# A two-block transformer on one core: fused convolution taps, a fixed engine for each weight half, and a planner that knows of the interface VectorE and GpSimd share

## The chip, the cores and the metric

The kernel runs on one core of one Trainium2 chip. A core has five engines that run side by side, each with its own queue of instructions: TensorE (PE in the profile, its weight loads PEld), VectorE (DVE), ScalarE (ACT), GpSimd (POOL) and SyncE (SP), which here only issues DMA transfers. The metric is device time of one execution in microseconds (us), lower is better; several runs are made and the median is taken.

## The reference

Two transformer blocks are computed in float32 on 512 tokens of width 1024. The parts that matter here:

```python
# block 1, the mixer's gated convolution: 256 channels, 31 taps along the tokens
y = a * sigmoid(g)
y = causal_dwconv(y, conv_w, conv_b)          # y[t] = b + sum_k w[k] * y[t - 30 + k]
y = silu(standardize(y by heads of 64) * gn_g + gn_b)
# beside it in the mixer: spatial gating (4 heads) and an mLSTM (4 heads), then
h = x + concat(y_a, y_b, y_c) @ w_out
# then cross attention, conv_glu (w_up, w_down); block 2: sparse attention with pooling,
# MLP, gated linear attention, MLP:
h = relu(h @ mlp_w1) ** 2 @ mlp_w2
...
```

The work is almost all products of 512-token activations with weight matrices. Every weight is read from memory once.

## The kernel before

**Products in three parts.** TensorE multiplies float32r operands, so each float32 matrix is held as two float32r parts, hi and lo, whose sum is exact (class `Split`), and a product is three matmuls: hi·hi, hi·lo and lo·hi (`mm`). For activations `split` makes hi with ScalarE (a copy that rounds) and lo with VectorE (source minus hi). In the trace these parts end in h and l: `xth`, `xtl` are activations, `wh`, `wl` weights, `hid` a hidden layer's pair.

**Weights.** `wunit` streams one unit of weights (128 x 1024) into a raw buffer `wr` (three of them) by DMA, and splits it by halves of 512 columns into two pages `wh` and `wl`. The kernel has 625 such halves. For them `split(..., weights=True)` leaves the engine open: `wh` may be a ScalarE copy or a VectorE cast, `wl = wr - wh` may be VectorE or GpSimd, with 1.0 us (`BIAS`) held against VectorE:

```python
nc.add([[("scalar", "activation", (hi, src, AF.Copy), {})], [("vector", "tensor_copy", (hi, src), {})]],
       BIAS)
self.either("tensor_sub", lo, src, hi.bitcast(F32), bias=BIAS)
```

Pages come free when the last matmul that reads them is done, and a stage may have only 5 to 9 units at a time (`rules`), so conversions are bound to TensorE's progress.

**Taps.** `taps` is the 31-tap convolution for two groups of 128 channels (`gcv`, from `yp`). For each tap but the first, a product `tm = yp * w` is made on VectorE or ScalarE (whichever the plan picks), and GpSimd adds it: `gcv += tm`. That is 60 products and 60 sums, sprinkled among the other steps of the mixer.

**What sets the order.** No engine order is written by hand. All calls go to a `Recorder`; `Plan` then lays the recorded steps out in time with a price for each instruction (`price1`) and a time until others see its result (`price`), tile space, DMA and activation tables. `Plan.run` takes at each point the engine that can start soonest, and on it the ready step of the highest rank; where a step has several forms (`either`, or `nc.add` with two lists), it takes the engine that by its prices is done first. `improve` repeats this eight times with the latest starts as ranks and keeps the shortest plan. `emit` then issues all instructions in the plan's order (one line, so nearly the whole trace bears line L487), and where the plan leaves TensorE idle for more than 1 us it adds products that nothing reads (`warm`, in the trace `ps<-ident`, 128x512) to fill the time. The program so fixed is static: on the chip each engine goes through its own list in order and waits on semaphores.

**Stages.** mix (the mixer, with keys and values of the memory, `mem`, as filler), xattn, ffn, nsa, mlp0, gla, mlp1. Each ends in a projection and a norm by token tiles (`tail`).

Of the kernel before, what the change touches and what calls it, by code (L numbers as in the profile page):

```python
# [28 lines left out]
# room: pages of weights or of a split block, half pages, weights on their way in  # L29
# [5 lines left out]
BIAS = 1.0  # L35


class Op:
    """One step of the plan: instructions that one engine issues back to back."""
# [20 lines left out]
def run(ap):  # L60
    """Elements next to each other in a transfer."""
    n = 1
    for s, k in sorted((int(s), int(k)) for s, k in list(ap.ap)[1:]):
        if s != n:
            break
        n *= k
    return n


def region(ap):  # L70
    """The tile, the partitions and the set of elements (as bits) that an access touches."""
# [26 lines left out]
class Recorder:  # L98
    """Stands in for the engines: keeps what they are told to do for the plan."""
# [9 lines left out]
    def add(self, forms, bias=0.0):  # L109
        """forms: ways to do one step, each a list of calls to one engine; bias: time against VectorE's."""  # L110
# [17 lines left out]
        o.forms = [(f[0][0], f) + price(f) + (bias if f[0][0] == "vector" else 0.0,) for f in forms]  # L128
# [3 lines left out]
    @contextmanager  # L132
    def together(self):
        """Calls to one engine as one step."""
        self.held = []
        yield
        calls, self.held = self.held, None
        self.add([calls])
# [11 lines left out]
def price1(eng, m, args, kw):  # L150
# [5 lines left out]
    if eng == "tensor":  # L156
        if m == "transpose":
            return 0.109
        if "float32r" in str(args[1].dtype):
            return max(n, 2 * width(args[1])) / 2400.0 + 0.0025  # L160
# [26 lines left out]

def price(calls):
    """Time on the engine, and the time after it until others see the result."""
# [5 lines left out]
class Plan:  # L195
    """Orders the recorded steps: each engine takes the ready step with the longest way to the end."""
# [16 lines left out]
    def depend(self):  # L213
# [29 lines left out]
        # weights wait for an earlier unit's end, and nothing starts too far ahead of its use  # L243
# [17 lines left out]
        # late banks are taken when all that goes into them is there  # L261
# [30 lines left out]
    def rank(self):  # L292
        for o in reversed(self.ops):
            eng, _, d, lat, _ = o.forms[0]
# [12 lines left out]
    def run(self, prio=None):  # L307
        ops, N = self.ops, len(self.ops)
        P = prio or [o.prio for o in ops]
        free = dict.fromkeys(Recorder.ENGINES, 0.0)  # L310
        dma_issue = dma_data = 0.0
# [17 lines left out]
        def room(o):  # L329
            """Time from which the step's new tiles find room; None if they may not be taken yet."""  # L330
# [32 lines left out]
        for _ in range(N):  # L363
            best = None
            for e, q in queue.items():
# [4 lines left out]
                for i in q:  # L370
                    o = ops[i]
                    s = ready[i] if ready[i] > f else f
                    if mn is not None and s > mn:
                        continue
                    form = next(x for x in o.forms if x[0] == e)
                    if len(o.forms) > 1:
                        mine = s + form[2] + form[4]
                        if any(max(ready[i], free[x[0]]) + x[2] + x[4] < mine - 1e-9 for x in o.forms if x[0] != e):
# [30 lines left out]
            _, calls, d, lat, _ = form  # L409
# [7 lines left out]
            else:  # L417
# [4 lines left out]
                end = free[e] = s + d  # L422
            o.start, o.end, o.pick, o.room = s, end, calls, taken
# [19 lines left out]
    def improve(self, n):  # L443
        """Plans again with the last plan's latest starts as ranks, and keeps the best plan."""
# [8 lines left out]
    def late(self):  # L453
        """Latest starts of the steps when each engine keeps its order, as priorities."""
# [16 lines left out]
    def emit(self, tc, warm):  # L471
        """warm: calls that keep the array's clock up, for a bank about to be used."""
# [17 lines left out]
class Split:  # L490
    """A float32 matrix as two float32r parts whose sum is exact."""
# [11 lines left out]
class Duo:  # L503
    """Two 128-row blocks of a split matrix, as one operand of the vector engines and as blocks."""
# [6 lines left out]
class Block:  # L511
# [19 lines left out]
    # ---- room  # L531
    def rules(self, quota, banks=(2, 10), pages=(2, 1000), halves=(0, 1000)):
        """For the steps from here on: units of weights at a time; of each kind of room, what a step ahead of
        its turn leaves free for those before it, and how many of them it may pass."""
# [3 lines left out]
    def ps(self, late=False):  # L538
        """A bank; late: not taken before all that goes into it is there."""
# [1336 lines left out]
```

## Time and profile before

| | |
|---|---|
| median of 3 runs | 2028.74 us (2028.26 to 2033.82) |
| profiled execution: span from first to last instruction | 2026.6 us |
| mean granted TensorE clock | 0.982 |
| busy: PE / DVE / ACT / POOL | 1931.1 / 1283.8 / 804.4 / 714.8 us |
| instructions on DVE / ACT / POOL | 2366 / 1614 / 571 |
| DMA | 177.40 MB, mean 88 GB/s |

"Busy" is the time in which at least one instruction of the engine runs. Matmuls are pipelined: one of 512 columns is shown some 0.39 us long while the next starts 0.23 us after it, so a hole between matmuls is longer in truth than the idle time shown. The profile page names groups as `out<-in`, by tile names without buffer numbers.

### The profile page before, as it was taken

The page shows a single profiled execution, that of the slowest core. Times are in us where ns is not written, and L with a number is a line of the kernel's source. Part 1 is how long each engine was busy: PE and PEld are TensorE (multiplying, and loading weights), DVE is VectorE, ACT ScalarE, POOL GpSimd, SP SyncE. Part 2 cuts the span into 40 slices and gives each one's busy share as a digit, 9 for nine tenths or more (in the row PEclk, how much of TensorE's full clock was granted, in tenths as well). Part 3 has the DMA queues.
Part 4 walks back from the last instruction along what each step waited for, and adds up shares of the span by engine and source line. Part 5 has one row for each costly group of instructions (what it writes and reads, how often), then busy time and mean ns, then how long its engine had stood idle before and what let it go on. Part 6 is the DMA issues. An engine that isn't in the chain of part 4 may idle for free. (4 is left out here: it accounts for less than half of the span.)

```text
span 2026.6 us, 27236 instructions
## 1 busy us (share of the span) xinstructions
PE 1931.1 (95%) x10206; PEld 1632.6 (81%) x10206; DVE 1283.8 (63%) x2366; ACT 804.4 (40%) x1614; POOL 714.8 (35%) x571
## 2 busy tenths in 40 slices
PE   8978899999999999989999999999999999999998
PEld 7756778888888888878888777777999888778776
DVE  5899966564444456588984345467686774355457
ACT  4556435334322233576734223232465334122231
POOL 3767534213212333233644222233223234122232
PEclk9988999999999999999999999999999999999999
DMA  5212333223213333330332233332223322223231
GB/s 165 79 47 72 125 94 115 83 63 105 74 54 102 115 101 89 70 74 11 97 112 84 63 94 104 85 126 77 83 62 104 94 73 87 61 77 107 91 127 55
DMA packets 215470, 177.40 MB, mean 88 GB/s; under 512 B 25174, under 2 KB 194202, under 8 KB 215338
## 3 DMA queue, kind: packets, MB, share of 16 engines
q1 hardware_dynamic: 215338, 175.66, 29.6%
q8 instruction: 80, 1.31, 0.3%
q14 instruction: 52, 0.43, 0.1%
HBM read 173.54 MB, written 2.10 MB: 87 GB/s over the span
## 5 line engine op out<-in xcount | busy, mean ns | idle before, releaser
L487 POOL TENSOR_TENSOR wl<-wr,wh 128x512 fp32r<-128x512 f32 (+1 forms) x387 | 551.7, 1438 | 1093.3 <-PE ps L487 450.3
L487 PE MATMUL ps<-xth,wl 128*128 128x512 f32 (+1 forms) x1464 | 516.9, 353 | 4.9 <-DVE wl L487 4.3
L487 PE MATMUL ps<-xtl,wh 128*128 128x512 f32 (+1 forms) x1464 | 517.3, 353 | 3.8 <-DVE xtl L487 3.7
L487 PE MATMUL ps<-xth,wh 128*128 128x512 f32 (+1 forms) x1464 | 519.4, 355 | 0.1
L487 ACT ACTIVATE wh<-wr 128x512 fp32r<-128x512 f32 (+1 forms) x544 | 311.9, 622 | 462.9 <-PE ps L487 277.3
L487 PE MATMUL ps<-wh,hid 128*128 128x512 f32 (+1 forms) x1392 | 437.5, 392 | 1.4 <-ACT wh L487 1.3
L487 DVE TENSOR_TENSOR wl<-wr,wh 128x512 fp32r<-128x512 f32 x238 | 285.0, 1211 | 135.4 <-ACT wh L487 78.9
L487 PEld LDWEIGHTS ps<-xth,wl 128*128 128x128 f32 x1464 | 278.3, 190 | 47.0 <-DVE wl L487 5.8
L487 PEld LDWEIGHTS ps<-xtl,wh 128*128 128x128 f32 x1464 | 278.6, 190 | 44.6 <-DVE xtl L487 6.0
L487 PEld LDWEIGHTS ps<-xth,wh 128*128 128x128 f32 x1464 | 279.0, 191 | 40.1 <-ACT xth L487 0.5
L487 PEld LDWEIGHTS ps<-wh,hid 128*128 128x128 f32 x1392 | 261.1, 188 | 60.9 <-ACT wh L487 2.7
L487 PE MATMUL ps<-wl,hid 128*128 128x512 f32 (+1 forms) x696 | 275.0, 395 | 7.7 <-DVE wl L487 6.2
L487 DVE TENSOR_TENSOR x<-x,ps 128x512 f32<-128x512 f32 (+1 forms) x210 | 140.6, 677 | 155.7 <-PE ps L487 154.8
L487 PEld LDWEIGHTS ps<-wl,hid 128*128 128x128 f32 x696 | 131.2, 188 | 46.5 <-DVE wl L487 13.6
L487 DVE TENSOR_TENSOR r<-r 128x512 f32<-128x512 f32 x64 | 69.0, 1079 | 65.2 <-ACT r L487 64.7
L487 DVE CAST wh<-wr 128x512 fp32r<-128x512 f32 x81 | 45.8, 581 | 90.5 <-PE ps L487 83.7
L487 PE MATMUL ps<-wl,xth 128*128 128x256 f32 (+2 forms) x320 | 94.6, 296 | 1.3 <-DVE wl L487 1.0
L487 PE MATMUL ps<-wh,xth 128*128 128x256 f32 (+2 forms) x320 | 95.7, 299 | 0.0
L487 PE MATMUL ps<-wh,xtl 128*128 128x256 f32 (+2 forms) x320 | 94.3, 295 | 0.0
L487 POOL TENSOR_TENSOR gcv<-gcv,tm 128x511 f32<-128x511 f32 (+29 forms) x60 | 81.4, 1376 | 16.8 <-DVE tm L487 12.3
L487 DVE TENSOR_TENSOR hid<-r,hid 128x512 fp32r<-128x512 f32 x64 | 51.8, 810 | 43.0 <-ACT hid L487 42.4
L487 ACT ACTIVATE r<-ps 128x512 f32<-128x512 f32 x64 | 37.7, 589 | 90.6 <-PE ps L487 90.6
(355 smaller groups left out, 2718.2 us busy)
## 6 DMA issues: line engine op xcount, KB each, us to landing
wr<-in_mlp_w_dram SPq DMA_DIRECT2D x128, 512.0 KB
wr<-in_w_up_dram SPq DMA_DIRECT2D x44, 512.0 KB
wr<-in_c_w_in_dram SPq DMA_DIRECT2D x24, 512.0 KB
wr<-in_w_down_dram SPq DMA_DIRECT2D x22, 512.0 KB
wr<-in_w_in_dram SPq DMA_DIRECT2D x16, 512.0 KB
wr<-in_w_xkv_dram SPq DMA_DIRECT2D x16, 512.0 KB
wr<-in_w_out_dram SPq DMA_DIRECT2D x8, 512.0 KB
wr<-in_w_xq_dram SPq DMA_DIRECT2D x8, 512.0 KB
```

The source lines that it names most:

```text
L487: getattr(getattr(self.rec.nc, eng), method)(*args, **kw)
```

## The change

Docstrings and comments are dropped too, which moves line numbers (L487 becomes L509) and nothing else. The rest:

```diff
-BIAS = 1.0
+BIAS = 0.0
...
-        o.forms = [(f[0][0], f) + price(f) + (bias if f[0][0] == "vector" else 0.0,) for f in forms]
+        o.forms = [(f[0][0], f) + price(f) + (bias if f[0][0] == "vector" else 0.0, port(f)) for f in forms]
...
         if "float32r" in str(args[1].dtype):
-            return max(n, 2 * width(args[1])) / 2400.0 + 0.0025
+            return max(n / 2285.0 + 0.007, width(args[1]) / 1200.0 + 0.0025)
...
+def port(calls):
+
+    for eng, m, args, kw in calls:
+        if eng not in ("vector", "gpsimd") or m in ("memset", "iota", "dma_start"):
+            continue
+        out = kw["out"] if "out" in kw else args[0]
+        ins = [x for x in list(args[1:]) + [x for k, x in kw.items() if k not in ("out", "accum_out")] if is_ap(x)]
+        room = [x for x in ins if "PSUM" not in str(x.space) and width(x) > 1]
+        if eng == "gpsimd" or len(room) > 1:
+            return True
+        if m in ("tensor_copy", "tensor_scalar") and room and "PSUM" not in str(out.space):
+            return True
+    return False
...
@@ Plan.run
+        shared = 0.0
...
+                    form = next(x for x in o.forms if x[0] == e)
+                    if form[5] and shared > s:
+                        s = shared
                     if mn is not None and s > mn:
                         continue
-                    form = next(x for x in o.forms if x[0] == e)
                     if len(o.forms) > 1:
                         mine = s + form[2] + form[4]
-                        if any(max(ready[i], free[x[0]]) + x[2] + x[4] < mine - 1e-9 for x in o.forms if x[0] != e):
+                        if any(max(ready[i], free[x[0]], shared if x[5] else 0.0) + x[2] + x[4] < mine - 1e-9
+                               for x in o.forms if x[0] != e):
                             continue
...
                 end = free[e] = s + d
+                if locks:
+                    shared = end
...
@@ Block.split, weights=True
-                nc.add([[("scalar", "activation", (hi, src, AF.Copy), {})], [("vector", "tensor_copy", (hi, src), {})]],
-                       BIAS)
-                self.either("tensor_sub", lo, src, hi.bitcast(F32), bias=BIAS)
+                nc.scalar.activation(hi, src, AF.Copy)
+                nc.vector.tensor_sub(lo, src, hi.bitcast(F32))
...
@@ taps
-                        tm = self.s2("tm")
-                        nc.add([[("vector", "tensor_scalar", (tm[:, :n], yp[j][:, :n], w, None), dict(op0=OP.mult))],
-                                [("scalar", "activation", (tm[:, :n], yp[j][:, :n], AF.Copy), dict(scale=w))]])
-                        nc.gpsimd.tensor_add(gcv[j][:, t:], gcv[j][:, t:], tm[:, :n])
+                        nc.vector.scalar_tensor_tensor(gcv[j][:, t:], yp[j][:, :n], w, gcv[j][:, t:], op0=OP.mult,
+                                                       op1=OP.add)
```

So three things change. A tap is one VectorE instruction, `gcv = yp * w + gcv`. Of every weight half `wh` is ScalarE's and `wl` VectorE's. And the planner has one more resource, `shared`: a GpSimd step, a VectorE step with two SBUF inputs, and a VectorE copy or scalar step from SBUF to SBUF hold it, and none of them starts while another holds it. A 512-column matmul is also priced a little dearer. Since all of the order comes from the plan, every engine's order changes.

By count over the whole program: `wl` on POOL 387 before, 0 now; on DVE 238, now 625. `wh` on ACT 544, now 625; on DVE 81, now 0. Taps: 40 products on DVE, 20 on ACT and 60 sums on POOL before; 60 fused instructions on DVE now. POOL has 576 instructions before and 128 now, DVE 2368 and 2692, ACT 1484 and 1543. The filler products on PE (`ps<-ident 128x512`) are 38 before and 180 now; of these 24 and 173 stand in the mix stage.

**First place: DVE and PE ahead of the first q product of the mixer.** `xconv` is the convolved input of an mLSTM head, made by DVE (its lo part) and taken by PE with `wh_165`, `wl_166` (the weights of q, k and v); `ps_168` is q's bank. DVE's rows up to `xconv`, before:

```order
L487 TENSOR_SCALAR tm_200<-yp_145,cols_78 128x509
L487 TENSOR_SCALAR tm_253<-yp_154,cols_78 128x504
L487 TENSOR_TENSOR wl_306<-wr_304,wh_305 128x384
L487 TENSOR_SCALAR tm_219<-yp_145,cols_78 128x508
L487 TENSOR_SCALAR tm_255<-yp_154,cols_78 128x503
L487 SCALAR_TENSOR_TENSOR gs_132<-gs_132,gs_133 4x512
L487 TENSOR_TENSOR xc_206<-ps_204,xc_206 128x512
L487 TENSOR_TENSOR xconv_140<-cv_138,xconv_140 128x512
```

and now:

```order
L509 SCALAR_TENSOR_TENSOR gcv_173<-yp_154,cols_78,gcv_173 128x491
L509 SCALAR_TENSOR_TENSOR gs_131<-gs_132,sm_49_124 4x512
L509 SCALAR_TENSOR_TENSOR gcv_173<-yp_154,cols_78,gcv_173 128x490
L509 SCALAR_TENSOR_TENSOR gcv_174<-yp_145,cols_78,gcv_174 128x497
L509 TENSOR_TENSOR gs_130<-gs_130,gs_131 4x512
L509 SCALAR_TENSOR_TENSOR gcv_173<-yp_154,cols_78,gcv_173 128x489
L509 SCALAR_TENSOR_TENSOR gcv_174<-yp_145,cols_78,gcv_174 128x496
L509 TENSOR_TENSOR xconv_140<-cv_138,xconv_140 128x512
```

From the last step of `cv_138` to `xconv_140` DVE had 12 instructions before; now it has 62, of which 39 are taps. PE's rows at the same product, before:

```order
L487 MATMUL ps_177<-wh_185,xth_86 128x512
L487 MATMUL ps_177<-wl_186,xth_86 128x512
L487 MATMUL ps_177<-wh_185,xtl_87 128x512
L487 MATMUL ps_168<-xconv_140,wh_165 128x512 x2
L487 MATMUL ps_168<-xconv_140,wl_166 128x512
L487 MATMUL ps_170<-xconv_140,wh_165 128x512 x2
```

and now:

```order
L509 MATMUL ps_176<-wh_206,xtl_91 128x512
L509 MATMUL ps_162<-ident,wsr_161 128x128 x4
L509 MATMUL ps_82<-ident,s_5_80 128x96
L509 MATMUL ps_168<-ident 128x512 x69
L509 MATMUL ps_168<-xconv_140,wh_165 128x512 x2
L509 MATMUL ps_168<-xconv_140,wl_166 128x512
L509 MATMUL ps_170<-xconv_140,wh_165 128x512 x2
```

The spatial gating's input projection (`ps_175` to `ps_178`) is now all ahead of q, and 69 fillers stand before it.

**Second place: weights in the last MLP.** At one point of mlp1 PE frees several pages at once and the next three units are converted. DVE before (with POOL's `wl` of the same units apart), `x` being the sum of the projection:

```order
L487 CAST wh_2618<-wr_2617 128x512
L487 CAST wh_2629<-wr_2628 128x512
L487 TENSOR_TENSOR wl_2616<-wr_2614,wh_2615 128x512
L487 TENSOR_TENSOR wl_2619<-wr_2617,wh_2618 128x512
L487 TENSOR_TENSOR wl_2630<-wr_2628,wh_2629 128x512
L487 TENSOR_TENSOR x<-x,ps_2627 128x512
```

DVE now (the unit numbers are lower by 60, the `tm` buffers that are gone):

```order
L509 TENSOR_TENSOR wl_2556<-wr_2554,wh_2555 128x512 x2
L509 TENSOR_TENSOR wl_2559<-wr_2557,wh_2558 128x512
L509 TENSOR_TENSOR wl_2570<-wr_2568,wh_2569 128x512 x2
L509 TENSOR_TENSOR x<-x,ps_2567 128x512
L509 TENSOR_TENSOR wl_2559<-wr_2557,wh_2558 128x512
```

The two casts went to ACT, and the three `wl` halves that stood on POOL here now stand in DVE's list.

More of the change, by code (lines that the diff above doesn't have):

```diff
@@ L293, in rank @@
         for o in reversed(self.ops):
-            eng, _, d, lat, _ = o.forms[0]
+            d, lat = o.forms[0][2:4]
+            eng = o.forms[0][0]
             o.prio = max((self.ops[s].prio for s in o.succs), default=0.0) + d + lat
@@ L408, in run @@
                     live[k].add(t)
-            _, calls, d, lat, _ = form
+            _, calls, d, lat, _, locks = form
             if e == "sync":
```

## The prediction

> **What bounds the kernel now.** I read the page's busy line first, then busy time by stretches of the span, then the waits of PE, then VectorE's and GpSimd's groups in the mixer, and last two stretches instruction by instruction.
>
> ```profile
> span 2026.6 us, 27236 instructions
> PE 1931.1 (95%) x10206; PEld 1632.6 (81%) x10206; DVE 1283.8 (63%) x2366; ACT 804.4 (40%) x1614; POOL 714.8 (35%) x571
> ```
>
> TensorE is busy 95% of the span. Its matmuls stay as they are, so what there is to win is its 95.5 us of idle time. By stretches (columns: length, busy time of PE, PEld, DVE, ACT, POOL, granted clock, DMA):
>
> ```profile
> 0.00:60.00 60.00, 51.33 (x345) 46.96 (x346) 31.27 (x76) 25.36 (x59) 19.27 (x27) 0.97 0.58 162
> 60.00:232.00 172.00, 139.98 (x737) 117.60 (x737) 166.53 (x372) 104.61 (x194) 121.65 (x104) 0.90 0.24 69
> 232.00:280.00 48.00, 44.61 (x190) 34.33 (x189) 39.59 (x109) 22.27 (x40) 17.88 (x13) 0.96 0.46 141
> 280.00:2000.00 1720.00, 1678.33 (x8845) 1419.14 (x8844) 1023.66 (x1758) 649.07 (x1317) 548.91 (x422) 0.99 0.29 85
> 2000.00:2026.60 26.60, 16.90 (x97) 14.60 (x95) 22.76 (x55) 3.05 (x4) 7.08 (x6) 0.86 0.21 79
> ```
>
> Three different limits. From 60 to 232 us, in the mixer, DVE is busy 166.5 of 172 us: there it is the bound, and PE has 32 of the 44.1 us that it idles up to 280. From 280 to 2000 PE is the bound, with 41.7 us of idle left in many small holes. The last 10 us are the final norm, which the change leaves alone.
>
> What fills DVE in the mixer (groups of DVE from 0 to 280 us; after the bar the busy time and the mean of one in ns):
>
> ```profile
> L487 DVE TENSOR_SCALAR tm<-yp,cols 128x509 f32<-128x509 f32 (+27 forms) x40 | 38.1, 975 | 0.8 <-POOL gcv L487 0.8
> L487 DVE TENSOR_TENSOR wl<-wr,wh 128x512 fp32r<-128x512 f32 (+1 forms) x33 | 32.7, 1004 | 11.1 <-ACT wh L487 10.9
> L487 DVE SCALAR_TENSOR_TENSOR sm<-sm,sm 128x1 f32<-128x1 f32 (+3 forms) x68 | 20.4, 309 | 0.6
> L487 DVE TENSOR_TENSOR sm<-sm,sm 128x4 f32<-128x4 f32 (+2 forms) x36 | 12.5, 353 | 0.3
> L487 DVE TENSOR_TENSOR sm<-sm 128x4 f32<-128x4 f32 (+3 forms) x34 | 11.4, 337 | 2.7 <-ACT nat L487 2.5
> L487 DVE TENSOR_SCALAR sm<-sm 128x1 f32<-128x1 f32 (+7 forms) x28 | 10.8, 386 | 0.2
> L487 DVE CAST wh<-wr 128x512 fp32r<-128x512 f32 x9 | 5.1, 595 | 5.6 <-PE ps L487 5.6
> ```
>
> An instruction on one to four columns that takes 0.3 us is odd. Over the whole trace the same kind has minimum/median/maximum:
>
> ```profile
> L487 DVE SCALAR_TENSOR_TENSOR sm<-sm,sm x257: 106/164/1327, 5.9 to 2022.0; 128x1 f32<-128x1 f32 x107, 128x4 f32<-128x4 f32 x17, 128x2 f32<-128x2 f32 x3, 128x8 f32<-128x8 f32 x2
> ```
>
> Its usual time is 0.164 us and its longest 1.327. The cause shows in the timeline (start, length; in brackets the idle time ahead), at the norm before ffn:
>
> ```profile
> 440.27 2.50 POOL L487 TENSOR_TENSOR wl<-wr,wh 128x512 fp32r<-128x512 f32 x2
> 440.36 2.42 DVE L487 SCALAR_TENSOR_TENSOR sm<-sm,sm 128x1 f32<-128x1 f32 x2
> 443.31 0.40 DVE L487 SCALAR_TENSOR_TENSOR sm<-sm,sm 128x1 f32<-128x1 f32 x2
> 444.65 0.63 PE L487 MATMUL ps<-ident,nat 128*128 128x128 f32 x4 [3.39 <-DVE nat L487]
> ```
>
> Beside two POOL sums two tiny DVE instructions take 2.42 us; with POOL silent, 0.40. And PE waits 3.39 us at the end of that chain. In mlp1:
>
> ```profile
> 1750.00 1.16 ACT L487 ACTIVATE wh<-wr 128x512 fp32r<-128x512 f32 x2 [24.64 <-PE ps L487]
> 1750.00 1.86 DVE L487 CAST wh<-wr 128x512 fp32r<-128x512 f32 x2 [8.14 <-PE ps L487]
> 1750.28 4.40 POOL L487 TENSOR_TENSOR wl<-wr,wh 128x512 fp32r<-128x512 f32 x3 [29.84 <-PE ps L487]
> 1751.79 4.04 DVE L487 TENSOR_TENSOR wl<-wr,wh 128x512 fp32r<-128x512 f32 x3
> 1753.59 0.50 PE L487 MATMUL ps<-wl,hid 128*128 128x512 f32 x1 [1.77 <-DVE wl L487]
> ```
>
> Two engines work on six `wl` halves and need from 1750.28 to 1755.83, 5.55 us, where DVE alone does three in 1.88:
>
> ```profile
> 1236.34 1.88 DVE L487 TENSOR_TENSOR wl<-wr,wh 128x512 fp32r<-128x512 f32 x3
> 443.75 1.42 DVE L487 SCALAR_TENSOR_TENSOR nat<-x,sm,g 128x512 f32<-128x512 f32 x2
> ```
>
> Together the pair manages one half in 0.93 us, DVE by itself one in 0.63, its own last 0.08 overlapping with what follows: 0.60 in a row. The second row is the nearest to a tap: scalar times tensor, then a second tensor, all in SBUF; two take 1.42, so 0.75 alone and 0.67 in a row.
>
> **The change part by part.** *Mixer, taps and `wl`: DVE's work.* DVE's busy time up to 280 us is 31.3 + 166.5 + 39.6 = 237.4 us. Removed: the 40 products, 38.1; the nine casts, 5.1. The 33 `wl`, 32.7, become all 82 of the stretch (POOL does 49, next fence) at 0.60 = 49.2. Added: 60 taps at 0.67, somewhat less as they shorten from 511 to 482 columns: 39. The four groups of tiny instructions, 55.1 us for 166, fall to 166 x 0.164 = 27.2 once POOL is quiet: 27.9 less. Sum: 237.4 - 38.1 - 5.1 - 32.7 + 49.2 + 39 - 27.9 = 221.8, so 15.6 us less, although DVE takes POOL's work over too. The other 20 products leave ACT. POOL's groups in the same stretch:
>
> ```profile
> L487 POOL TENSOR_TENSOR gcv<-gcv,tm 128x511 f32<-128x511 f32 (+29 forms) x60 | 81.4, 1376 | 16.8 <-DVE tm L487 12.3 <-DVE sm L487 2.5 <-ACT tm L487 1.8
> L487 POOL TENSOR_TENSOR wl<-wr,wh 128x512 fp32r<-128x512 f32 (+1 forms) x49 | 65.7, 1352 | 91.4 <-ACT wh L487 66.6 <-PE ps L487 20.1 <-DVE sm L487 2.8
> ```
>
> and the old products by minimum/median/maximum:
>
> ```profile
> L487 DVE TENSOR_SCALAR tm<-yp,cols x40: 459/1106/1575, 66.5 to 205.7; 128x509 f32<-128x509 f32 x2, 128x505 f32<-128x505 f32 x2, 128x504 f32<-128x504 f32 x2, 128x503 f32<-128x503 f32 x2
> ```
>
> A tap's price is not in the trace; from above it is bounded by POOL's contended sum, 1.376 (then 60 taps cost 83, and the saving turns into a loss of 28 us), from below by the product alone at its minimum, 0.459, since a tap does that and a sum (28 us, 11 more to gain). I take 0.67, the same operation on the same shape. Where DVE is the bound, its 15.6 us come off the end.
>
> The Trainium skill, "SBUF — State Buffer", section "Who interferes with whom", says that a VectorE instruction with two SBUF inputs and a GpSimd one that reads SBUF exclude each other for a whole instruction. The trace agrees: 3 sums of POOL, 1.25 each, and 3 of DVE at 0.60 make 5.55 us, which is what 1750.28 to 1755.83 took. By that rule taps and `wl`, all with two SBUF inputs, can still be held up by what POOL keeps in the mixer.
>
> *What POOL keeps* there is 13 tensor sums of 128 to 512 columns (pieces of the score rows, one `cv`) in the new order; at 1.25 us for the largest about 12 us. They cost DVE between nothing (where it reads PSUM meanwhile, or idles) and 12. I take 4, since DVE had to do some of these itself before.
>
> *Mixer, PE.* The new plan leaves PE more planned holes: 149 further fillers in this stage. One lasts as long as the step from one 512-column matmul to the next:
>
> ```profile
> 77.33 0.39 PE L487 MATMUL ps<-wh,xtl 128*128 128x512 f32 x1
> 77.56 0.40 PE L487 MATMUL ps<-xconv,wh 128*128 128x512 f32 x1
> 82.33 0.79 PE L487 MATMUL ps<-xconv,wh 128*128 128x512 f32 x1 [4.37 <-DVE xconv L487]
> ```
>
> 0.23 us, so 34 us in all. They stand in idle time that is there anyway and so cost nothing while the holes last; if a hole is shorter than its fillers they hold PE up. Idle in this stretch is 44.1 us, in truth more, since each hole hides another 0.16 us (0.39 shown against 0.23) and short stalls do not show. So at most some 15 to 25 us can go. The place shown first fits: between the last step of `cv` and `xconv` DVE has 62 instructions of about 0.6 us, 37 us, in place of 12 of up to 1 us, so `xconv` comes some 25 us later; PE puts the gating projection ahead of it, and its hole of 4.4 us still becomes 16 (69 x 0.23). PE's loss there must come back later, where taps no longer stand in its way. DVE's sum gives 15.6 - 4 = 12 us, PE's holes allow 15 to 25; I take 14 from the whole mixer, bounds 0 and 25.
>
> *After 280 us.* PE's waits there:
>
> ```profile
> PE ps L487 <- DVE nat L487: 8.6, 6, 3.4
> PE ps L487 <- DVE wl L487: 8.4, 14, 1.8
> PE ps L487 <- DVE xtl L487: 3.0, 5, 1.2
> PE ps L487 <- DVE q L487: 2.9, 1, 2.9
> PE ps L487 <- POOL wl L487: 2.3, 5, 0.8
> ```
>
> All five end in work that shares the interface. At 1750 ACT makes the next halves at 0.58 each in a row and DVE follows at 0.60; the `wl` for which PE waited until 1753.59 comes second in that line, some 1.44 us after 1750 and not 3.5, and the hole of 1.77 closes. At 440 the chain of tiny instructions loses 2 us of PE's 3.39. The `wl` waits (10.7) go; I give norms and the rest half, and add 0.16 for each of some 55 holes closed wholly or in part: about 30 of 41.7 + 9. Bounds: 11 if only the `wl` waits go; 45 if nearly all does. DVE's added 387 `wl` are 232 us; what it sheds outside the mixer is larger than it looks, because 205 `wl` that took 1.2 us on the mean take 0.6. DVE stays near 60% busy, so it covers them. The 81 more `wh` on ACT (0.58 each, 47 us) lie beside PE in an engine busy 40%; without that cover they would delay the `wl` behind them by up to 1.2 us for a unit. Fewer waits mean that pages come free a little sooner, and DMA at 29% has room.
>
> *The planner's new rule and prices* issue nothing; their effect is the order, priced above. The dearer matmul moves fillers and ranks only.
>
> Sum: 2026.6 - 14 - 30 = 1982.6 us of span; the median of the runs lies 2.1 us above this profile's span, so 1985 us.
>
> **The rivals.** *More than this:* holes close nearly everywhere, 25 + 45: 1959. It needs norms that do not hold PE up, against which speaks that `nat` waits on a chain of DVE steps with or without POOL. *Only one half works:* the mixer gains nothing (POOL's last 12 us fall on DVE, or a head's chain is late) or the rest gains only its `wl` waits: 2028.7 - 30 = 1999 to 2028.7 - 14 - 11 = 2004, both weak 2018. *No change:* idle time moves to other waits as fast as it goes, 2022 to 2035; for it speaks that DVE, not POOL, already releases most of PE's waits. *Slower:* the mixer becomes longer. DVE's list is in order, 39 taps stand ahead of the first `xconv`, and q, the scores and the values of four heads follow from it one after another. If the chain and not DVE's total sets the mixer's end, the 34 us of fillers are new idle time: 2028.7 + 34 - 30 = 2033, and 2052 if the rest gains only 11. It decides once PE's idle and fillers up to the end of `mem` exceed 44 + 30 us. Against it: DVE idles 5.5 us in 172, so it is the total that binds. *The change does not do what it says* is ruled out by the order: no `wl` is left on POOL.
>
> **The numbers.** My forecast (1965 to 1998) 0.58; more than this 0.09; one half 0.18; no change 0.07; slower 0.08. Differences below 0.3%, some 6 us, cannot be told from none. Faster: 0.58 + 0.09 + 0.18 = 0.85; same 0.07; slower 0.08. A range of 8 in 10 takes the forecast, the half and part of the larger gain: 1958 to 2014.
>
> **What would show it.** POOL's busy time falls from 715 to some 100 us; tiny `sm` instructions have a mean near 0.17 and `wl` near 0.68 with no 1.7 left; DVE total 1180 to 1260; the stretch to the end of `mem`'s products (280 us now) ends at 262 to 270, with a hole or fillers of some 16 us before the first `xconv` product; PE's waits for `wl` after it below 3 us. I would be wrong if taps last over 0.9 us, if the mixer ends after 280, or if PE's waits at the norms grow because DVE now has `wl` queued ahead of the norm's steps.

## The result, and the profile after

The changed kernel takes 1964.07 us (median of 4 runs, 1962.58 to 1966.51), the one before 2029.67; ratio 0.9674, 95% interval 0.966 to 0.9687. Faster by 65.6 us; the forecast was some 44 us. In the profiled executions the span falls from 2026.6 to 1962.6 us. The page's first lines:

```profile
span 1962.6 us, 26913 instructions
PE 1930.5 (98%) x10348; PEld 1645.3 (84%) x10348; DVE 1214.9 (62%) x2690; ACT 824.2 (42%) x1673; POOL 78.5 (4%) x123
```

TensorE's busy time is the same as before (1931.1), with 142 more filler products in it. What has gone is idle time, and some of the length that the other products show: the clock in the mixer is higher (next rows), and products that follow one another without a hole overlap in the profile. By the stretches that the prediction used (length, busy PE, PEld, DVE, ACT, POOL, clock, DMA):

```profile
60.00:232.00 172.00, 169.10 (x923) 143.82 (x922) 157.58 (x482) 100.49 (x193) 18.23 (x29) 0.98 0.29 85
232.00:280.00 48.00, 48.00 (x209) 39.00 (x208) 28.02 (x60) 17.16 (x35) 0.00 (x0) 1.00 0.33 108
280.00:2000.00 1720.00, 1657.39 (x8836) 1411.29 (x8834) 992.25 (x2051) 673.21 (x1375) 57.26 (x79) 0.99 0.30 86
```

PE is busy 169 of 172 us in the mixer, where it was 140, and the granted clock there is 0.98, where it was 0.90. (1720 us are asked for in the last row; the span ends at 1962.6.)

A point that both orders have divides the span: the last product of `mem`, in the row of PE's products `ps<-wh,mt` (minimum/median/maximum, first and last start).

```profile
L487 PE MATMUL ps<-wh,mt x64: 387/393/774, 225.3 to 274.6; 128*128 128x512 f32 x64
L509 PE MATMUL ps<-wh,mt x64: 388/395/477, 212.1 to 252.3; 128*128 128x512 f32 x64
```

It ends at 275.0 us before and 252.7 now: 22.3 us from the mixer (the forecast took 14), and 41.7 from all that follows, which falls from 1751.6 to 1709.9 (the forecast took 30). All of the stretch up to there, before and after:

```profile
0.00:275.00 275.00, 230.92 (x1246) 194.88 (x1247) 232.39 (x548) 150.79 (x291) 157.41 (x143) 0.93 0.35 102
0.00:252.70 252.70, 245.80 (x1395) 211.75 (x1396) 204.27 (x596) 142.91 (x281) 21.19 (x44) 0.99 0.37 108
```

VectorE does 28.1 us less although `wl` and the taps are now all its own. Its groups in that stretch (busy, mean in ns), to be held against the seven of the prediction:

```profile
L509 DVE TENSOR_TENSOR wl<-wr,wh 128x512 fp32r<-128x512 f32 (+1 forms) x80 | 52.6, 690 | 18.5 <-ACT wh L509 10.8 <-PE ps L509 7.0
L509 DVE SCALAR_TENSOR_TENSOR gcv<-yp,cols,gcv 128x511 f32<-128x511 f32 (+29 forms) x60 | 40.9, 719 | 0.0
L509 DVE SCALAR_TENSOR_TENSOR sm<-sm,sm 128x1 f32<-128x1 f32 (+3 forms) x68 | 11.2, 174 | 0.4
L509 DVE TENSOR_TENSOR sm<-sm 128x4 f32<-128x4 f32 (+3 forms) x34 | 5.9, 179 | 3.1 <-ACT nat L509 2.9
L509 DVE TENSOR_TENSOR sm<-sm,sm 128x4 f32<-128x4 f32 (+2 forms) x36 | 5.2, 150 | 0.2
L509 DVE TENSOR_SCALAR sm<-sm 128x1 f32<-128x1 f32 (+7 forms) x28 | 4.0, 151 | 0.1
```

The same 166 tiny steps took 55.1 us and take 26.3. At the norm before ffn, where PE waited 3.39 us behind them, the timeline now reads:

```profile
414.45 0.22 DVE L509 SCALAR_TENSOR_TENSOR sm<-sm,sm 128x1 f32<-128x1 f32 x1
414.58 0.69 DVE L509 TENSOR_TENSOR wl<-wr,wh 128x512 fp32r<-128x512 f32 x1
415.18 0.16 DVE L509 SCALAR_TENSOR_TENSOR sm<-sm,sm 128x1 f32<-128x1 f32 x1
415.38 1.42 DVE L509 SCALAR_TENSOR_TENSOR nat<-x,sm,g 128x512 f32<-128x512 f32 x2
416.27 0.63 PE L509 MATMUL ps<-ident,nat 128*128 128x128 f32 x4 [0.21 <-DVE nat L509]
```

The planner slips a `wl` between two steps of the chain, and PE's wait is 0.21. The place in mlp1 where two engines needed 5.55 us for six halves of `wl`:

```profile
1691.45 3.10 DVE L509 TENSOR_TENSOR wl<-wr,wh 128x512 fp32r<-128x512 f32 x5 [8.11 <-PE ps L509]
1691.68 2.20 ACT L509 ACTIVATE wh<-wr 128x512 fp32r<-128x512 f32 x4 [24.72 <-PE ps L509]
1694.47 0.68 DVE L509 TENSOR_TENSOR x<-x,ps 128x512 f32<-128x512 f32 x1
1695.07 0.69 DVE L509 TENSOR_TENSOR wl<-wr,wh 128x512 fp32r<-128x512 f32 x1
```

Six halves and an `x` between them in 4.31 us, on DVE alone, and no wait of PE. Of the waits that the prediction named, PE still has these over the whole span (total, times, longest); a wait for `q` is no longer listed:

```profile
PE ps L509 <- DVE wl L509: 5.1, 10, 1.3
PE ps L509 <- DVE nat L509: 1.6, 3, 1.2
PE ps L509 <- DVE xtl L509: 1.4, 4, 0.5
```

### The profile page after: what moved, and what is told of

It is laid out like the page before. It is cut to its first block, busy times and chain, and to the rows that moved or that the text cites. A ratio compares the mean times of both kernels' runs of the same rounds, so it can differ in the third digit from the quotient of the medians.

```text
span 1962.6 us, 26913 instructions
## 1 busy us (share of the span) xinstructions
PE 1930.5 (98%) x10348; PEld 1645.3 (84%) x10348; DVE 1214.9 (62%) x2690; ACT 824.2 (42%) x1673; POOL 78.5 (4%) x123
## 4 chain that ended last, share of the span: by engine, by line
PE 86%; DVE 9%; ACT 3%; DMA 2%; issue 1%; SPq 0%; POOL 0%; DVEq 0%; ACTq 0%
PE ps L509 86%; DVE wl L509 2%; DVE sm L509 1%; DVE gcv L509 1%; ACT wh L509 1%; ACT p L509 1%; DMA wr<-in_mlp_w_dram 1%; DVE xtl L509 0%; DVE x L509 0%; DVE pt L509 0%; DMA wr<-in_w_up_dram 0%; ACT xth L509 0%; DMA g<-in_norm_mix_g_dram 0%; DMA wr<-in_w_down_dram 0%; DMA wr<-in_a_w_out_dram 0%
## 5 line engine op out<-in xcount | busy, mean ns | idle before, releaser
L509 ACT ACTIVATE wh<-wr 128x512 fp32r<-128x512 f32 x625 | 357.1, 623 | 423.5 <-PE ps L509 271.5
L509 DVE TENSOR_TENSOR wl<-wr,wh 128x512 fp32r<-128x512 f32 x625 | 406.2, 686 | 205.6 <-PE ps L509 96.8
L509 PE MATMUL ps<-xth,wh 128*128 128x512 f32 (+1 forms) x1464 | 516.9, 353 | 0.4 <-ACT hg L509 0.4
L509 PE MATMUL ps<-xtl,wh 128*128 128x512 f32 (+1 forms) x1464 | 514.4, 351 | 1.4 <-DVE xtl L509 1.4
L509 PE MATMUL ps<-xth,wl 128*128 128x512 f32 (+1 forms) x1464 | 513.4, 351 | 0.0
L509 PE MATMUL ps<-wh,hid 128*128 128x512 f32 (+1 forms) x1392 | 436.4, 391 | 1.8 <-ACT wh L509 1.7
L509 PEld LDWEIGHTS ps<-wh,hid 128*128 128x128 f32 x1392 | 260.3, 188 | 61.6 <-ACT wh L509 3.3
L509 PEld LDWEIGHTS ps<-xtl,wh 128*128 128x128 f32 x1464 | 276.2, 189 | 41.4 <-DVE xtl L509 2.6
L509 PEld LDWEIGHTS ps<-xth,wh 128*128 128x128 f32 x1464 | 276.4, 189 | 40.2 <-ACT xth L509 0.8
L509 PEld LDWEIGHTS ps<-xth,wl 128*128 128x128 f32 x1464 | 275.7, 188 | 39.9 <-DVE wl L509 0.2
L509 PE MATMUL ps<-wl,hid 128*128 128x512 f32 (+1 forms) x696 | 272.4, 391 | 1.6 <-DVE wl L509 1.5
L509 DVE TENSOR_TENSOR x<-x,ps 128x512 f32<-128x512 f32 (+1 forms) x210 | 141.1, 678 | 162.8 <-PE ps L509 162.2
L509 PEld LDWEIGHTS ps<-wl,hid 128*128 128x128 f32 x696 | 130.8, 188 | 34.2 <-DVE wl L509 4.8
L509 DVE TENSOR_TENSOR r<-r 128x512 f32<-128x512 f32 x62 | 42.8, 691 | 99.8 <-ACT r L509 99.7
L509 PE MATMUL ps<-wl,xth 128*128 128x256 f32 (+2 forms) x320 | 94.4, 295 | 3.4 <-DVE wl L509 3.4
L509 PE MATMUL ps<-wh,xth 128*128 128x256 f32 (+2 forms) x320 | 94.7, 296 | 0.0
L509 PE MATMUL ps<-wh,xtl 128*128 128x256 f32 (+2 forms) x320 | 93.9, 293 | 0.0
L509 ACT ACTIVATE r<-ps 128x512 f32<-128x512 f32 x64 | 38.0, 593 | 114.9 <-PE ps L509 114.9
L509 DVE SCALAR_TENSOR_TENSOR cv<-ps,cols,cv 128x511 f32<-128x511 f32 (+2 forms) x56 | 41.8, 746 | 39.1 <-ACT cv L509 38.5
L509 PEld LDWEIGHTS ps<-wl,xth 128*128 128x128 f32 x320 | 60.4, 189 | 5.6 <-DVE wl L509 4.2
L509 PE MATMUL ps<-wh,o 128*128 128x512 f32 x192 | 62.3, 394 | 0.0
L509 PEld LDWEIGHTS ps<-wh,xth 128*128 128x128 f32 x320 | 60.3, 189 | 1.4
```

What stands on the lines that cost most here:

```text
L509: getattr(getattr(self.rec.nc, eng), method)(*args, **kw)
```

## Experiments

"End of `mem`" is the end of the products named above, in the profiled execution; "rest" is the span from there; DVE and POOL are their busy time up to there. Ratios are against the kernel before on the same chip.

| kernel | time, us | ratio (95%) | end of `mem` | rest | DVE | POOL |
|---|---|---|---|---|---|---|
| before | 2029.7 | 1 | 275.0 | 1751.6 | 232.4 | 157.4 |
| changed | 1964.1 | 0.9674 (0.966 to 0.9687) | 252.7 | 1709.9 | 204.3 | 21.2 |
| 1 taps only | 2031.4 | 1.0017 (1.0003 to 1.003) | 277.4 | 1751.5 | 212.1 | 106.2 |
| 2 weights only | 1991.6 | 0.9811 (0.9795 to 0.9827) | 284.7 | 1706.6 | 221.3 | 99.5 |
| 3 planner only | 1974.5 | 0.9728 (0.9714 to 0.9743) | 256.6 | 1713.4 | 211.3 | 110.2 |
| 4 taps and weights | 1967.9 | 0.9696 (0.9681 to 0.971) | 258.4 | 1706.5 | 206.6 | 26.9 |
| 5 added reads on GpSimd | 2107.1 | 1.0378 (1.0362 to 1.0393) | 277.1 | 1828.4 | 238.7 | 132.8 |
| 6 added writes on GpSimd | 1981.5 | 0.9755 (0.9741 to 0.977) | 259.4 | 1720.4 | 204.8 | 140.6 |
| 7 half the taps | 1944.6 | 0.9575 (0.9561 to 0.9589) | 233.4 | 1710.9 | 183.7 | 28.9 |
| 8 no fillers | 1969.8 | 0.9703 (0.9687 to 0.9719) | 260.1 | 1705.9 | 205.3 | 21.6 |
| 9 8 taps on TensorE | 1954.6 | 0.9636 (0.9621 to 0.965) | 244.6 | 1708.3 | 195.5 | 17.7 |
| 10 12 taps on TensorE | 1955.7 | 0.9636 (0.962 to 0.9652) | 245.2 | 1711.1 | 190.9 | 14.6 |
| 11 weights and planner | 1981.5 | 0.9767 (0.9753 to 0.9782) | 273.3 | 1710.0 | 191.7 | 91.4 |
| 12 old matmul price | 1967.9 | 0.9698 (0.9684 to 0.9713) | 261.0 | 1703.5 | 203.6 | 24.8 |

**Theory and rival.** Theory: GpSimd's reads of SBUF hold the interface that VectorE's two-input steps need; taking `wl` and the sums off GpSimd sets VectorE free, and its total is what the mixer waits for. Rival: the new order brings the gain, or `wl` is faster merely because DVE is the faster engine.

### The parts one by one (runs 1 to 4)

Run 1 is the kernel before with the new `taps` alone, run 2 with the fixed engines of `split` alone, run 4 with both, all three with the old planner. Run 3 has the new planner rule, price and `BIAS = 0.0` alone, with the old taps and the weights left open:

```diff
  # runs 1, 2 and 4: the planner does not know of the interface, and a matmul has its old price
  def port(calls):
+     return False
  # run 3: weights open to both engines, taps as a product and a GpSimd sum
- nc.vector.tensor_sub(lo, src, hi.bitcast(F32))
+ self.either("tensor_sub", lo, src, hi.bitcast(F32), bias=BIAS)
```

> The kernel before with one part of the change alone: the 60 fused taps on VectorE; weight halves and planner as before. In the order POOL keeps 394 wl halves and loses the 60 tap sums. Exclusion theory (VectorE and GpSimd hold each other up, and whatever takes reading work off GpSimd gains): only the mixer changes, its 60 sums leave POOL but 49 wl there stay; end of the memory's products (275 us before) at 260 to 272, nothing after it; 2014 to 2026 us. Plan theory (the order made with wrong times is what costs): no gain or a loss, 2024 to 2045, since fused taps are added to the bounding engine without the planner knowing of the interface. Tap theory (the mixer is most of the gain): 1985 to 2005.

> The kernel before with one other part alone: wh always on ScalarE, wl always on VectorE; taps (60 sums on POOL) and planner as before. Exclusion theory: the 42 us won after the mixer come whole, the mixer gains a part (49 halves off POOL, 60 sums stay): 1975 to 1992 us; waits of TensorE for wl after 280 us under 4 us. Plan theory: 2005 to 2025, since the planner still does not know of the interface. Tap theory: 2005 to 2020.

> The planner's part alone: the shared resource, the dearer matmul and the bias of 0, with both forms of a weight half still open and the taps as products and GpSimd sums. By its order it leaves 83 of 387 wl on POOL and all 60 tap sums. Exclusion theory: it gains by what it moves off POOL, so most of the gain after the mixer and less in it: 1978 to 1998 us. Plan theory: nearly the whole gain, 1962 to 1976. Rival that the planner's part does nothing: 2024 to 2034.

> Both edits of the code (fused taps, fixed engines for the weight halves) with the planner of before: no shared resource, old price of a matmul. No wl on POOL by the order. Exclusion theory: within 8 us of the changed kernel, 1958 to 1972, since little that could clash is left for the planner to know of. Plan theory: 1985 to 2010.

The rest of the kernel is settled by this: with `wl` off GpSimd (runs 2 and 4) it takes 1706.5 us, with the taps alone it does not move. That the planner's knowledge alone (run 3) brings it to 1713 is no counter-case, since the plan then leaves only 83 of 625 `wl` halves on GpSimd.

The mixer is not a sum of parts: taps alone move its end by +2.4 us, weights alone by +9.7, both together by -16.6. The planner's part alone (run 3) moves it by -18.4, most of the changed kernel's 22.3, although all 60 tap sums are still on GpSimd, which is busy 110 us there; of the 48 `wl` that it had in this stretch it keeps 12. So in the mixer the gain does not need the sums off GpSimd: a plan that moves `wl` and places the sums otherwise can bring most of it. In run 1 DVE loses 20.3 us of work and nothing comes off the end. What holds the mixer up in run 1 is not settled: PE's largest single wait there is 4.4 us, behind `pl` on POOL, and its clock in the mixer is 0.95.

### The taps under the new planner (run 11)

```diff
- nc.vector.scalar_tensor_tensor(gcv[j][:, t:], yp[j][:, :n], w, gcv[j][:, t:], op0=OP.mult, op1=OP.add)
+ nc.add([[("vector", "tensor_scalar", (tm[:, :n], ...))], [("scalar", "activation", (tm[:, :n], ...))]])
+ nc.gpsimd.tensor_add(gcv[j][:, t:], gcv[j][:, t:], tm[:, :n])
```

> The changed kernel with the taps of before (product on VectorE or ScalarE, sum on GpSimd); fixed engines for the weights and the planner's new rule stay. If the mixer's gain needs the sums off GpSimd (theory, since 60 sums of 1.25 us hold the interface for 75 us): mem ends at 262 to 280 us, the rest stays at 1704 to 1712 us, 1970 to 1988 us. If it is enough that the planner knows of the interface (rival, as planner alone brought the mixer to 256.6 us): mem ends at 250 to 258 us, 1960 to 1968 us.

The mixer ends at 273.3, as the theory had it, but not because of VectorE's total, which at 191.7 us is lower than in the changed kernel. The timeline shows another cause:

```profile
125.64 25.25 POOL L509 TENSOR_TENSOR gcv<-gcv,tm 128x498 f32<-128x498 f32 x23 [2.35 <-ACT tm L509]
150.85 0.53 POOL L509 TENSOR_SCALAR_AFFINE_SELECT pw<-pw 128x128 f32<-128x128 f32 x2
151.17 1.16 DVE L509 TENSOR_TENSOR pw<-ps,pw 128x512 f32<-128x512 f32 x2 [27.60 <-POOL pw L509]
151.92 1.65 PE L509 MATMUL ps<-ident 128*128 128x512 f32 x3 [27.95 <-DVE pw L509]
```

The mask of the first score rows (`pw`) is a GpSimd step. It stands in POOL's list behind 23 tap sums, DVE waits 27.6 us for it at the head of its list, and PE 27.95 us behind DVE. Run 2 has a hole of the same kind, 21.5 us of PE at `DVE pw`, where 11 sums in 13.0 us stand ahead of the mask. With the taps on DVE the sums are out of POOL's list. The taps bring 20.6 us from run 11 to the changed kernel, less than this one hole. So under the new planner it is most likely GpSimd's queue that they relieve, while the prediction had reckoned with the interface alone. Where the plan puts the sums matters too: in run 3, with the same 60 sums and the same planner rule, PE's longest wait in the mixer is 3.1 us.

### Work put back on GpSimd (runs 5 and 6)

The lists of PE, DVE and ACT are those of the changed kernel, instruction for instruction. Only GpSimd gets something to do behind each `wh`, into a scratch tile that nobody reads:

```diff
+ if eng == "scalar" and args[0].tensor.name.startswith("wh"):
+     pool.tensor_sub(r[:, 0:n], h[:, 0:n], h[:, 0:n])                 # run 5: reads 480 columns twice
+     pool.tensor_copy(r[:, 0:1], h[:, 0:1])                           # run 6: one column, then only writes
+     pool.memset(r[:, 0:480], 0.0); pool.memset(r[:, 0:480], 0.0)
```

> The changed kernel with one instruction more per weight half on GpSimd, behind the making of wh: a tensor subtraction of 480 columns that reads wh twice and writes to a scratch tile that nobody reads (some 1.16 us each, 625 of them, about 720 us). The planner does not know of it; the lists of TensorE, VectorE and ScalarE are the same as in the changed kernel, instruction for instruction. If the gain comes from GpSimd no longer holding the shared interface (theory): wl again 0.9 to 1.3 us on the mean, tiny sm instructions up to 1.3 us again, and the time goes back to 2020 to 2120 us, 60 us or more above the changed kernel; VectorE's 1215 us and GpSimd's 720 us, which exclude each other for the most part, add up to almost the whole span. If the gain came from the order of the new plan or from wl being made on a faster engine (rival): 1964 to 1975 us, since nobody waits for the added instructions but the pages that they read.

> As the run with added reads, but the added work on GpSimd writes instead: behind each wh a copy of one column of it and two memsets of 480 columns of the scratch tile (together some 1 us, 625 times). Lists of TensorE, VectorE and ScalarE again the same. If it is reading on GpSimd that excludes VectorE (theory): within 6 us of the changed kernel, 1960 to 1970 us, wl at 0.69 us on the mean. If any work of GpSimd in SBUF slows VectorE, or if the later release of pages and GpSimd's own steps behind the added ones is what costs (rival): as slow as the run with added reads, 2010 us or more.

GpSimd's added instructions and DVE's `wl` and tiny groups over the whole span, run 5 and then run 6:

```profile
L513 POOL TENSOR_TENSOR scr<-wh 128x480 f32<-128x480 f32 x617 | 756.1, 1225 | 1020.2 <-ACT wh L509 987.9 <-ACT misc L509 0.4
L509 DVE TENSOR_TENSOR wl<-wr,wh 128x512 fp32r<-128x512 f32 x625 | 600.0, 997 | 158.5 <-PE ps L509 76.5 <-ACT wh L509 61.1 <-issue 17.6
L509 DVE SCALAR_TENSOR_TENSOR sm<-sm,sm 128x1 f32<-128x1 f32 (+3 forms) x257 | 78.4, 310 | 3.7
PE ps L509 <- DVE wl L509: 42.5, 45, 3.4
```

```profile
L513 POOL MEMSET scr<- 128x480 f32 x625 | 313.1, 501 | 37.1
L509 DVE TENSOR_TENSOR wl<-wr,wh 128x512 fp32r<-128x512 f32 x625 | 404.2, 684 | 208.3 <-ACT wh L509 95.7 <-PE ps L509 72.7 <-POOL scr L514 22.4
L509 DVE SCALAR_TENSOR_TENSOR sm<-sm,sm 128x1 f32<-128x1 f32 (+3 forms) x257 | 47.7, 191 | 3.7
PE ps L509 <- DVE wl L509: 5.1, 10, 1.3
```

This is the clearest comparison of the study. With reads on GpSimd, `wl` goes from 0.686 to 0.997 us on the mean, the tiny steps from 0.188 to 0.310, PE's waits for `wl` from 5.1 to 42.5 us, and the time to 2107, worse than the kernel before. With writes, although GpSimd is busy even longer (918 us against 853), `wl`, the tiny steps and PE's waits for `wl` stay as in the changed kernel. So with one and the same order on the other engines, and every `wl` on VectorE, the time moves by 143 us: neither the new order nor the faster engine is enough while GpSimd reads beside VectorE. What share of the mixer's gain is the order's, these two runs do not tell (run 3 is the case to look at).

GpSimd's writes are not without effect on VectorE, which the theory did not give. Steps that copy or scale one SBUF tile into another get longer, for instance `qf` (minimum/median/maximum, changed kernel and then run 6):

```profile
L509 DVE TENSOR_SCALAR qf<-qf,sm x16: 272/280/288, 1421.6 to 1522.5; 128x128 f32<-128x128 f32 x16
L509 DVE TENSOR_SCALAR qf<-qf,sm x16: 276/284/648, 1433.0 to 1533.9; 128x128 f32<-128x128 f32 x16
```

At 1427.56 us of run 6 a copy of four columns takes 0.53 us beside a memset of 0.50, where the longest such copy of the changed kernel takes 0.171. Such steps are few here: VectorE's busy time is 1218.0 us against 1214.9.

Run 6 is still 17.4 us slower than the changed kernel. A part of this is that GpSimd's own steps come late behind the added ones: PE's waits for them (`p`, `x`, `pl`) go from 1.4 to 8.7 us. The rest is not settled. So of run 5's 143 us a part, perhaps of the order of run 6's 17, is GpSimd's queue and not the interface.

The Trainium skill, "SBUF — State Buffer", section "Who interferes with whom", says that a VectorE instruction with two SBUF inputs contends with a GpSimd instruction that reads SBUF, and not with one that only writes it. The two runs show both halves of that sentence.

### What sets the mixer's end in the changed kernel (runs 7, 9 and 10)

Run 7 leaves out 15 of the 31 taps of each group, so it does less than the reference; runs 9 and 10 make all, the first 8 or 12 of each group on TensorE:

```diff
- for t in range(31):                                                  # run 7
+ for t in range(16):
+ if t < 8:                                                            # run 9; 12 in run 10
+     nc.scalar.activation(d, self.ident, AF.Copy, scale=w)            # diagonal matrix of the tap
+     nc.tensor.matmul(acc[j][:, t:], d, yp[j][:, :n], start=t == 0, stop=t == 7)
+     if t == 7:
+         nc.scalar.activation(gcv[j], acc[j], AF.Identity, bias=col["conv_b_b"][:, j:j + 1])
```

> The changed kernel with 16 of the 31 taps of the convolution (the other 15 of each group of channels are left out): 30 instructions of VectorE fewer in the mixer, 30 x 0.69 = 21 us of its work. If VectorE's total sets the mixer's end (what the prediction took): the last product of mem comes 12 to 21 us sooner than 252.7 us, time 1943 to 1952 us. If a chain of steps of the heads sets it (rival): mem ends within 5 us of 252.7, time 1958 to 1968 us; the fillers ahead of the first q product change in number with the plan.

> The changed kernel with the first 8 taps of each group made on TensorE: 16 float32 products of a diagonal matrix (one column of weights on the identity, made by ScalarE) with yp, summed in one bank; ScalarE takes the bank out with the bias, so VectorE has 14 taps fewer, 14 x 0.72 = 10 us. If VectorE's total sets the mixer's end in the changed kernel (theory, after the run with half the taps): the last product of mem comes 7 to 10 us sooner than 252.7 us, 1953 to 1959 us, and the 16 products, for which fillers make room, cost TensorE nothing. If TensorE's own list or a chain of steps binds (rival): no gain, and up to 16 x 0.9 = 14 us lost, 1962 to 1978 us.

> As before with 12 taps of each group on TensorE: 22 taps fewer on VectorE, 16 us, and 24 float32 products, some 21 us of TensorE. VectorE's total as the bound: mem ends 10 to 16 us sooner, 1948 to 1956 us. Rival: the products are longer than the holes that they replace, so less is gained than with 8, 1957 to 1970 us.

Up to the end of `mem`, run 7 and run 9:

```profile
0.00:233.40 233.40, 221.13 (x1293) 189.73 (x1294) 183.66 (x567) 139.15 (x277) 28.94 (x45) 1.00 0.40 117
0.00:244.60 244.60, 233.05 (x1314) 195.06 (x1314) 195.52 (x585) 147.20 (x294) 17.74 (x41) 0.99 0.37 108
```

DVE's busy time falls by 20.6 us and the end comes 19.3 sooner; by 8.8 and the end comes 8.1 sooner. In the changed kernel VectorE's total does set the mixer's end, almost one for one. Run 7 carries this reading; run 9's 8.1 us fit it, but run 12 will show that another plan alone can move the end as much. Run 9 computes all of it and is, with run 10, the best version here: 1954.6 us, 9.5 less than the changed kernel. Its 16 products, each in two records on PE:

```profile
L509 PE MATMUL ps<-yp,dg x32: 587/590/592, 51.6 to 67.6; 128*128 128x512 f32 x4, 128*128 128x511 f32 x4, 128*128 128x510 f32 x4, 128*128 128x509 f32 x4
```

They lie where the changed kernel has fillers, of which the plan has 60 up to the end of `mem` in place of 173. With 12 taps there (run 10) DVE sheds 13.4 us, but the end moves by only 7.5: the first q product comes at 100.1 us, in run 9 at 93.7, so the total is no longer the only bound. What holds it back is not settled.

### The fillers (run 8)

```diff
- if o.room is not None and o.start - last > self.IDLE:
+ if False and o.room is not None and o.start - last > self.IDLE:
```

> The changed kernel without its 180 filler products on TensorE (180 x 0.23 = 41 us of PE time), the rest of the order the same. If the fillers stand in idle time that is there anyway and the clock does not need them (what the prediction took for the first part): 1960 to 1967 us with holes in place of fillers. If some holes are shorter on the chip than planned, so that fillers hold products up: mem ends 3 to 14 us sooner, 1950 to 1961 us. If the granted clock falls behind the holes: below 0.95 in the stretch 60 to 232 us, mem ends later than 252.7, 1967 to 1985 us.

At the place ahead of the first q product, the changed kernel and then run 8:

```profile
80.20 15.94 PE L509 MATMUL ps<-ident 128*128 128x512 f32 x69
95.98 0.89 PE L509 MATMUL ps<-xconv,wh 128*128 128x512 f32 x2
```

```profile
81.39 0.47 PE L509 MATMUL ps<-xconv,wh 128*128 128x512 f32 x1
97.56 0.80 PE L509 MATMUL ps<-xconv,wh 128*128 128x512 f32 x1 [15.69 <-DVE xconv L509]
```

The hole is there without fillers, 15.69 us long, so the 69 fillers stand in true idle time. But PE's clock (the column before the DMA share) falls within it in run 8, and is still at half some 10 us after products have resumed:

```profile
84.00:88.00 4.00, 0.00 (x0) 0.83 0.77 248
88.00:92.00 4.00, 0.00 (x0) 0.50 0.01 2
104.00:108.00 4.00, 4.00 (x15) 0.50 0.43 121
112.00:116.00 4.00, 4.00 (x18) 1.00 0.00 0
```

The mixer ends 7.4 us later, the whole takes 5.8 us more. The third of the expected cases holds, in the stretch from 60 to 232 us with a clock of 0.87 against 0.98.

### Another plan of the same work (run 12)

```diff
- return max(n / 2285.0 + 0.007, width(args[1]) / 1200.0 + 0.0025)
+ return max(n, 2 * width(args[1])) / 2400.0 + 0.0025
```

> The changed kernel with the planner's old price of a matmul (0.216 us for 512 columns in place of 0.231); no instruction differs, only the plan's order and fillers. If that price means nothing by itself: within 5 us of the changed kernel, 1959 to 1969 us; the difference is then also a measure of what another plan of the same work is worth. If the dearer matmul is what made the plan better (rival): mem ends over 5 us later or the rest over 5 us longer, 1970 us or more.

3.8 us slower, so the price brings little. But the mixer ends 8.3 us later and the rest is 6.4 us shorter: where the plan puts work around the end of `mem` shifts a few us between the two parts. By this one sample, single figures of the table's two columns are good to some 8 us, their sum to some 4, when the plan differs; run 1's +2.4 us and run 9's -8.1 are within that. Run 4's 3.8 us to the changed kernel is of the same size, so what the planner's new rule adds once both code edits are made is not told apart from another plan.

## Why the prediction was right, and where its sizes were off

*Direction* held, and after the mixer so did the mechanism; in the mixer it is borne out in part (below). The time is 1964.07 where 1985 was named. That is inside the range, but 0.9 us below the likeliest case (1965 to 1998) and so on the side of the rival "more than this" (1959), which had a chance of 0.09. What that rival needed came true: norms hardly hold PE up now (`nat`, 0.4 us). Against it stood that `nat` waits on a chain of DVE steps with or without POOL; the chain is still there, but its steps are short.

*Mixer, 14 us taken, 22.3 measured.* The term mis-sized is DVE's sum. Its parts that were worked out came out close: tiny steps -28.8 (27.9 forecast), `wl` from 32.0 to 52.6 us (49.2 forecast), taps 40.9 (39); with the old products and casts gone, these make -9.1 us. DVE's real change is -28.1. The other 19 us lie in groups that the sum left alone. Some 8 of them are steps that the new plan no longer gives to DVE: pieces of the score rows (`pl`, `phl`) that went to GpSimd, and three of ten `hn`. The other 11 are, nearly all, steps of the same number that became shorter, which fits the interface; the sum took only the tiny ones as held up. One group of each kind, before and after, with POOL's `pl` after:

```profile
L487 DVE TENSOR_TENSOR pl<-pw,ph 128x512 fp32r<-128x512 f32 (+2 forms) x10 | 5.1, 520 | 0.0
L487 DVE SCALAR_TENSOR_TENSOR za<-za,sm,gb 128x256 f32<-128x256 f32 x8 | 6.7, 846 | 0.0
L509 POOL TENSOR_TENSOR pl<-pw,ph 128x512 fp32r<-128x512 f32 (+2 forms) x10 | 9.8, 995 | 34.1 <-ACT ph L509 34.1
L509 DVE SCALAR_TENSOR_TENSOR za<-za,sm,gb 128x256 f32<-128x256 f32 x8 | 3.8, 485 | 0.0
```

The 4 us taken for what POOL keeps point the other way, and cost nothing that shows: `wl` is at 0.690 us on the mean in this stretch, where 0.68 was expected for the whole.

*"Where DVE is the bound, its 15.6 us come off the end"* is right for the changed kernel (run 7, and run 9 with it) and was argued from the wrong place: 20 us less on DVE brought nothing in run 1, in runs 2 and 11 the largest hole is behind GpSimd's queue, and run 3 ends the mixer at 256.6 us with 7 us more on DVE than the changed kernel. A 97% busy DVE was not proof that its total alone bound the old mixer. That the mixer gained as forecast, and more, is thus partly luck: the prediction gave the planner's new rule no gain of its own.

*Fillers at nothing* was right for the hole (16 us forecast, 15.94 filled, 15.69 without) but left out what they bring: they keep the clock up. Without them (run 8) the mixer's end comes 7.4 us later, and its gain is 14.9 us.

*After 280 us, 30 taken, 41.7 measured.* That the gain comes from `wl` off GpSimd is shown by runs 2 and 4 (45 us) and by run 5. Two sizes were off, in opposite directions. PE's waits for `wl`, which were to go wholly, fell from 10.7 to 5.1 us; one that is left shows a reason:

```profile
1515.69 1.28 ACT L509 ACT_TABLE_LOAD   x1
1517.10 0.62 ACT L509 ACTIVATE wh<-wr 128x512 fp32r<-128x512 f32 x1
1519.34 1.28 DVE L509 TENSOR_TENSOR wl<-wr,wh 128x512 fp32r<-128x512 f32 x2
1520.08 0.38 PE L509 MATMUL ps<-wl,xth 128*128 128x256 f32 x1 [1.15 <-DVE wl L509]
```

`wh` now always queues behind ScalarE's other steps, here a table load, and `wl` behind a norm's chain on DVE; the prediction had priced that at nothing. The other waits, of which half was taken, closed almost wholly: `nat` from 8.6 us to 0.4 after the mixer, `xtl` from 3.0 to 1.4, and `q` from 2.9 to less than 0.3.

*What was to be seen.* POOL 78.5 us (some 100 forecast), DVE's total 1214.9 (1180 to 1260), `wl` at 0.686 on the mean (0.68) and the tiny steps at 0.188 (0.17); the fillers before the first `xconv` product span 15.94 us (some 16). Three signs were missed. The longest `wl` is still 1.789 us, against "no 1.7 left". PE's waits for `wl` after the mixer are 5.1 us, not below 3. And the end of `mem` was named as 280 us before and 262 to 270 after; it is 275.0 and 252.7.

*The rivals.* "Slower" named the queue on DVE: 39 taps ahead of the first `xconv`. It did delay DVE's part of `xconv`, from 81.1 to 95.7 us, but DVE's later work, rid of the taps, made up for it. "Only one half works" is near what the weights alone were (run 2: 1991.6 us, the mixer's end 9.7 us later).

## What to carry to other kernels

An engine that helps out can cost more than it does. Where two engines exclude each other, add up what every group of the other engine takes in excess of its undisturbed time, not only the groups that look odd. Then look at what stands in the helper's own queue: a short mask behind 23 long sums cost TensorE 28 us. And when VectorE's total is the bound, look for idle time on TensorE that is being filled with products nobody reads; 14 taps put there brought another 9.5 us. And try the plan's part by itself: here the planner's part alone (run 3) gave some 55 of the 66 us; with it the plan takes most of the weight work off GpSimd.

## What the runs showed of the hardware that was not expected

What holds VectorE up depends on its step. Two-input steps suffer from GpSimd's reads and not from its writes: 1250 memsets on GpSimd left `wl` at 0.684 us on the mean, while 625 subtractions that read made it 0.997. Copies and scalings from SBUF to SBUF suffered from the memsets too: the longest `qf` went from 0.288 to 0.648 us, and the mean of the copies `x<-nat` from 0.416 to 0.525. In run 8 TensorE's clock was at 0.50 some 6 us into a hole, and about 14 us passed from the first product after the hole until a 4-us stretch read 1.00 again.
